# A channel shuffle in 44 DMAs: the first two buffers of each pool filled in small pieces

## The chip, the cores and the metric

The kernel runs on one core of a Trainium2 chip. The core has several engines with instruction streams of their own. Here VectorE (DVE in the profile) copies, SyncE (SP) issues the loads, ScalarE (ACT) issues the stores, and 16 DMA engines move the bytes of both. The metric is the device time of one execution in microseconds; the time before is the median of six runs.

## What is computed

The input holds 16 x 64 x 64 = 65,536 rows of 256 channels in float32, 64 MB. In each row the channels are seen as 8 groups of 32, and the two axes are exchanged: a channel shuffle, a pure move of data with no arithmetic.

```python
batch, h, w, c = x.shape                      # 16, 64, 64, 256
channels_per_group = c // groups              # 256 // 8 = 32
x = x.reshape(batch, h, w, groups, channels_per_group)
x = x.transpose(0, 1, 2, 4, 3)
x = x.reshape(batch, h, w, c)
```

Every byte is read from the chip's memory once and written once: 67.11 MB each way.

## The kernel before

The input is taken as one flat array. It is cut into consecutive chunks of 128 x q rows. Each of the 128 partitions of the on-chip memory gets q consecutive rows, that is q KB, since a row of 256 float32 is 1 KB. The list `_SIZES` (line 12) says which q are used: 4, 8, 16, then fifteen times 32, then 4. So there are 19 chunks, of 512 KB (q = 4), 1 MB, 2 MB, and 4 MB (q = 32) in all.

One loop runs over the chunks, and each pass does three things:

- line 47: SP issues one DMA that loads the chunk into `in_tile`;
- line 49: VectorE copies `in_tile` to `out_tile` with the two axes exchanged, through strided views;
- line 53: ACT issues one DMA that stores `out_tile` to the output.

`in_tile` comes from a pool of three buffers and `out_tile` from another pool of three. Every buffer has room for the largest chunk, 32 KB in each partition, and a chunk takes a whole buffer however small it is. Buffers are handed out in turn. So the load of chunk i waits until chunk i - 3 has been copied out of its input buffer, and the copy of chunk i waits until the store of chunk i - 3 has landed, besides the load of chunk i itself.

The order of the instructions is that of the loop (line 43 asks for a manual schedule); each engine goes through its own in that order. SP has 19 loads and ACT 19 stores, each 128 partitions by 1024, 2048, 4096 or 8192 float32 elements. The waits go over semaphores that the framework hands out: a completion semaphore for each DMA, taken in turn from a set of eight for loads and stores together, and one that counts VectorE's copies. A semaphore is used again for a later DMA, and the engine that issues that DMA waits first until the earlier one on the same semaphore has landed.

Of the kernel before, what the change touches and what calls it, by code (L numbers as in the profile page):

```python
# [1 line left out]

# [4 lines left out]


F32 = mybir.dt.float32
P = 128  # L10

_SIZES = [4, 8, 16] + [32] * 15 + [4]
_IN_BUFS = 3
_OUT_BUFS = 3


@with_exitstack
def kernel(
    ctx: ExitStack,
    tc: tile.TileContext,  # L20
    x: bass.AP,
    groups: bass.AP,
    out: bass.AP,
):
    nc = tc.nc
    b, h, w, c = x.shape
    G = int(groups)
    CPG = c // G
    assert G * CPG == c
    assert sum(_SIZES) * P == b * h * w  # L30
    biggest = max(_SIZES)

    x_flat = x.rearrange("b h w c -> (b h w c)")
    out_flat = out.rearrange("b h w c -> (b h w c)")

    in_pool = ctx.enter_context(tc.tile_pool(name="in_pool", bufs=_IN_BUFS))
    out_pool = ctx.enter_context(tc.tile_pool(name="out_pool", bufs=_OUT_BUFS))

    def rows(flat, first, q):

        return flat[first * c : (first + P * q) * c].rearrange("(p f) -> p f", p=P)

    ctx.enter_context(tc.manual_schedule(engines=None))
    first = 0
    for q in _SIZES:
        in_tile = in_pool.tile([P, biggest * c], F32, name="in_tile")
        nc.sync.dma_start(out=in_tile[:, : q * c], in_=rows(x_flat, first, q))  # L47
        out_tile = out_pool.tile([P, biggest * c], F32, name="out_tile")
        nc.vector.tensor_copy(  # L49
            out=out_tile[:, : q * c].rearrange("p (i j g) -> p i j g", j=CPG, g=G),  # L50
            in_=in_tile[:, : q * c].rearrange("p (i g j) -> p i j g", g=G, j=CPG),
        )
        nc.scalar.dma_start(out=rows(out_flat, first, q), in_=out_tile[:, : q * c])
        first += P * q


# [1 line left out]
_INS = ['x', 'groups']  # L58
_OUTS = [((16, 64, 64, 256), 'float32')]

_NUMBERS = {'groups': 8}


# [26 lines left out]
```

## Time and profile before

| | us |
|---|---|
| median of six runs | 316.74 (316.66 to 317.0) |
| the profiled execution | 316.7 |
| its span in the profile | 314.9 |
| VectorE busy, 19 copies | 120.1 |
| a copy of 128 x 8192 (32 KB), mean of 15 | 7.473 |
| a copy of 128 x 4096 / 2048 / 1024 | 3.841 / 2.010 / 1.096 |
| a 4 MB load from issue to landing, median | 50.5 |
| a 4 MB store from issue to landing, median | 42.1 |

The profile follows one execution. The span runs from its first to its last recorded event; the execution's own time is 1.8 us longer. Queue q1 carries the loads and q10 the stores. A transfer is cut into packets, one for each partition and a small one of 4 bytes for the completion on each of the 16 DMA engines, and the trace has a record of each packet with its size, start and duration. 5,472 packets in all move 134.22 MB, at a mean of 426 GB/s over the span. Times from issue to landing include the time that a transfer stands in its queue behind earlier ones.

### The profile page before, as it was taken

What the parts mean: (1) busy time and instruction counts of PE and PEld (TensorE: products, weight loads), DVE (VectorE), ACT (ScalarE), POOL (GpSimd) and SP (SyncE); (2) the same over time, 40 slices, a digit from 0 to 9 for tenths busy, and PEclk for the clock granted to TensorE, in tenths of its full rate; (3) what the DMA queues carried; (4) which work ended last, traced back from release to release, by engine and by line L of the source; (5) the groups of instructions that cost most, each with busy time, mean ns of one, the idle gap of its engine ahead of it and who ended that gap; (6) DMA issues with size and microseconds to landing.
All of it is one profiled execution on the core that took longest, in us unless ns stands there. A gap on an engine that the chain in (4) does not pass through costs nothing.

```text
span 314.9 us, 150 instructions
## 1 busy us (share of the span) xinstructions
DVE 120.1 (38%) x19; POOL 0.2 (0%) x4
## 2 busy tenths in 40 slices
DVE  3409270905318062170722608136080450905500
POOL 0000000000000000000000000000000000000000
DMA  8999999999999999999999999999999999999997
GB/s 318 405 427 444 408 458 404 462 404 462 404 462 404 462 404 462 404 462 404 466 400 466 400 466 400 466 400 466 400 466 400 466 400 466 400 466 427 439 400 333
DMA packets 5472, 134.22 MB, mean 426 GB/s; under 512 B 608, under 2 KB 608, under 8 KB 1120
## 3 DMA queue, kind: packets, MB, share of 16 engines
q1 hardware_dynamic: 2736, 67.11, 49.9%
q10 hardware_dynamic: 2736, 67.11, 49.4%
HBM read 67.11 MB, written 67.11 MB: 426 GB/s over the span
## 4 chain that ended last, share of the span: by engine, by line
DMA 40%; another core or an unknown queue 30%; DVE 25%; issue 0%; DVEq 0%; SPq 0%
DMA in_tile<-in_x_dram 40%; DVE out_tile L49 25%; DVEq L49 0%; SPq L47 0%
## 5 line engine op out<-in xcount | busy, mean ns | idle before, releaser
L49 DVE COPY out_tile<-in_tile 128x8192 f32<-128x8192 f32 (+3 forms) x19 | 120.1, 6323 | 179.2 <-DMA in_tile<-in_x_dram 179.2
L71 POOL MEMSET const-bfloat16-1.0<- 128x1 bf16 x1 | 0.1, 102 | 0.0
L71 POOL MEMSET const-uint8-127<- 128x1 uint8 x1 | 0.1, 102 | 0.0
L71 POOL MEMSET const-float32-0.0<- 128x1 f32 x1 | 0.1, 99 | 0.2 <-issue 0.2
L71 POOL MEMSET const-float32-1.0<- 128x1 f32 x1 | 0.1, 99 | 0.0
## 6 DMA issues: line engine op xcount, KB each, us to landing
in_tile<-in_x_dram SPq DMA_DIRECT2D x15, 4096.0 KB, 50.5
out_dram<-out_tile ACTq DMA_DIRECT2D x15, 4096.0 KB, 42.1
in_tile<-in_x_dram SPq DMA_DIRECT2D x1, 2048.0 KB, 11.0
out_dram<-out_tile ACTq DMA_DIRECT2D x1, 2048.0 KB, 29.9
in_tile<-in_x_dram SPq DMA_DIRECT2D x2, 512.0 KB, 22.6
in_tile<-in_x_dram SPq DMA_DIRECT2D x1, 1024.0 KB, 5.2
out_dram<-out_tile ACTq DMA_DIRECT2D x2, 512.0 KB, 14.4
out_dram<-out_tile ACTq DMA_DIRECT2D x1, 1024.0 KB, 23.2
```

The source lines that it names most:

```text
L49: nc.vector.tensor_copy(out=out_tile[:, : q * c].rearrange("p (i j g) -> p i j g", j=CPG, g=G), in_=in_tile[:, : q * c].rearrange("p (i g ...
L71: nc = _bacc.Bacc("TRN2", target_bir_lowering=False, num_devices=1)
```

## The change

`_SIZES` is replaced by `_SLOTS`, a list of buffers, each with a list of pieces. The first buffer of each pool is shared by six pieces of 4, 4, 4, 4, 8 and 8 KB per partition, the second by two of 16 KB, and fourteen more tiles of 32 KB follow. The small chunk at the end is gone. Each piece still has its own load, its own copy and its own store, on a part of the columns of the shared tiles. There are 22 of each, so 44 DMAs instead of 38.

Within one buffer the loop now issues all loads of its pieces first, and then goes through the pieces once more, with the copy and the store of each. A buffer is free for the tile that takes it next when all its pieces are done.

```diff
-_SIZES = [4, 8, 16] + [32] * 15 + [4]
+_SLOTS = [[4, 4, 4, 4, 8, 8], [16, 16]] + [[32]] * 14
...
-    for q in _SIZES:
+    for parts in _SLOTS:
         in_tile = in_pool.tile([P, biggest * c], F32, name="in_tile")
-        nc.sync.dma_start(out=in_tile[:, : q * c], in_=rows(x_flat, first, q))
         out_tile = out_pool.tile([P, biggest * c], F32, name="out_tile")
-        nc.vector.tensor_copy(
-            out=out_tile[:, : q * c].rearrange("p (i j g) -> p i j g", j=CPG, g=G),
-            in_=in_tile[:, : q * c].rearrange("p (i g j) -> p i j g", g=G, j=CPG),
-        )
-        nc.scalar.dma_start(out=rows(out_flat, first, q), in_=out_tile[:, : q * c])
-        first += P * q
+        at = 0
+        pieces = []
+        for q in parts:
+            pieces.append((q, first, slice(at * c, (at + q) * c)))
+            first += P * q
+            at += q
+        for q, start, cols in pieces:
+            nc.sync.dma_start(out=in_tile[:, cols], in_=rows(x_flat, start, q))
+        for q, start, cols in pieces:
+            nc.vector.tensor_copy(
+                out=out_tile[:, cols].rearrange("p (i j g) -> p i j g", j=CPG, g=G),
+                in_=in_tile[:, cols].rearrange("p (i g j) -> p i j g", g=G, j=CPG),
+            )
+            nc.scalar.dma_start(
+                out=rows(out_flat, start, q), in_=out_tile[:, cols]
+            )
```

In the built program of the changed kernel SP issues the loads in the order of the list, 1024 elements x4, 2048 x2, 4096 x2 and 8192 x14, VectorE copies and ACT stores in the same order. The first five loads wait for nothing. The sixth uses the semaphore of the second. The seventh and eighth (16 KB) and the ninth (the first of 32 KB) use the semaphores of the first, second and third store, and so wait for these to land.

More of the change, by code (lines that the diff above doesn't have):

```diff
@@ L29 @@
     assert G * CPG == c
-    assert sum(_SIZES) * P == b * h * w
-    biggest = max(_SIZES)
+    assert sum(map(sum, _SLOTS)) * P == b * h * w
+    biggest = max(map(sum, _SLOTS))
     x_flat = x.rearrange("b h w c -> (b h w c)")
```

## The prediction

> **What bounds the kernel now.** I read first the page's busy shares and its two DMA rows, then the same in stretches, then the ends of the run instruction by instruction.
>
> ```profile
> span 314.9 us, 150 instructions
> ...
> DVE 120.1 (38%) x19; POOL 0.2 (0%) x4
> ...
> DMA  8999999999999999999999999999999999999997
> GB/s 318 405 427 444 408 458 404 462 404 462 404 462 404 462 404 462 404 462 404 466 400 466 400 466 400 466 400 466 400 466 400 466 400 466 400 466 427 439 400 333
> ...
> q1 hardware_dynamic: 2736, 67.11, 49.9%
> q10 hardware_dynamic: 2736, 67.11, 49.4%
> ```
>
> The only engine that computes is busy 38% of the span. The two DMA queues, loads (q1) and stores (q10), fill 49.9% + 49.4% = 99.3% of the 16 DMA engines' time between them. The alternation 404/462 is only a beat of 4 MB transfers against slices.
>
> ```profile
> 1.70:5.00 3.30, 1.08 (x1) 0.00 (x0) 1.00 1.00 382
> 5.00:10.00 5.00, 2.03 (x2) 0.00 (x0) 1.00 1.03 388
> ...
> 100.00:260.00 160.00, 60.83 (x9) 0.00 (x0) 1.00 1.00 434
> 260.00:298.00 38.00, 14.97 (x2) 0.00 (x0) 1.00 1.01 435
> ...
> 312.00:314.90 2.90, 0.00 (x0) 0.00 (x0) 1.00 0.43 175
> ```
>
> (Columns: stretch, length, VectorE, GpSimd, clock, DMA share, GB/s.) The middle runs at 434 GB/s with a DMA share of 1.00. Below that rate are only the first microseconds and the last. So the kernel is bound by DMA work from its first packet (1.74 us in the packet records) to its last (313.66 us). VectorE's waits for loads cost nothing in themselves, as the DMA engines work through them.
>
> ```profile
> DVE out_tile L49 <- DMA in_tile<-in_x_dram: 179.2, 19, 12.0
> ...
> 3.92 1.09 DVE L49 COPY out_tile<-in_tile 128x1024 f32<-128x1024 f32 x1 [3.92 <-DMA in_tile<-in_x_dram]
> ...
> 5.05 57.66 ACTq L53 DMA_DIRECT2D out_dram<-out_tile  x6
> ...
> 287.25 7.51 DVE L49 COPY out_tile<-in_tile 128x8192 f32<-128x8192 f32 x1 [11.86 <-DMA in_tile<-in_x_dram]
> 298.24 1.10 DVE L49 COPY out_tile<-in_tile 128x1024 f32<-128x1024 f32 x1 [3.46 <-DMA in_tile<-in_x_dram]
> ```
>
> The first store is issued at 5.05 us. After the last copy, at 299.3 us, 14 us of stores still stand in the queue.
>
> **The account in packets.** A transfer gives each of the 16 engines 8 packets (128 partitions / 16), one per partition, and a 4-byte completion. Single packet records of this trace have a median of 0.159 us for 4 KB, 0.309 for 8 KB, 0.611 for 16 KB, 1.213 for 32 KB and 0.009 for the completion; thus some 0.009 us of a packet does not scale with its size. One engine's work in one direction before: 16 x 0.159 + 8 x 0.309 + 8 x 0.611 + 120 x 1.213 + 19 x 0.009 = 155.6 us, both directions 311.3. The page says 99.3% of 314.9 = 312.7 busy. The 1.4 us between are packets over their median, nearly all loads, and the records say when: 0.3 us up to 2.5 us (first accesses), 0.6 us from 5.5 to 9.9 us (16 KB loads with no store beside them, about 0.75 instead of 0.611 each), 0.5 us from 19 to 36 us (32 KB loads beside 8 and 16 KB stores), almost none later.
>
> **The change, part by part.**
>
> *More and smaller packets.* After: 32 x 0.159 + 16 x 0.309 + 16 x 0.611 + 112 x 1.213 + 22 x 0.009 = 155.9, both directions 311.7 us: +0.45. In the steady middle a 32 KB packet costs 32768 x 16 / 434 GB/s = 1.208 us, not 1.213, and 16 of these go: +0.08. Together +0.5 us; ends 0.4 and 0.6.
>
> The Trainium skill has a rule against this change ("DMA: Bandwidth & Descriptors", sections "Anatomy of one DMA" and "Rules for kernel authors"): about 2.0 us fixed per DMA, measured on the software-generated path, and at least 1 MiB each for bandwidth. Six more DMAs would be 12 us by it if nothing overlapped, 328.7 us in all; the packet records above have 9 ns per packet, because other transfers fill the wait.
>
> *The head.* Loads of 4, 4, 4, 4 and 8 KB go out unhindered. The first copy and store keep their rows (3.92 and 5.05 us), the next pieces follow at the pace of their loads (8 x 0.159 = 1.3 us against 1.09 us of copy). No transfer starts sooner than now, and there is no idle DMA to fill except the 1.74 us before the first packet, which stays.
>
> *The 16 KB loads no longer run alone.* Reads ahead of them: 32 x 0.159 + 16 x 0.309 = 10.0 us, from 1.74 + 0.3 on, so not before 12 us. The first store's packets begin between 6.1 (its issue plus the 1.0 us that the first load took from issue at 0.73 to packet at 1.74) and 9.1 us (where they began before). Up to then loads are of 4 and 8 KB, which ran at their median before. I take the 0.6 us off; ends 0 and -0.6.
>
> *The mix lasts longer.* The engines alternate one store packet with one load packet: the 512 KB store below takes 14.1 us to land, 8 packets of its own beside 16 and 32 KB loads.
>
> ```profile
> out_dram<-out_tile ACTq DMA_DIRECT2D x1, 512.0 KB, 14.1
> ```
>
> (The same page, section "Queues, rings and completion order", lets an engine drain a whole packet of about 9 to 17 descriptors before it switches; by that the 8 would go in one turn. The total would be the same by both.) Small stores before are 24 packets per engine, and 32 KB loads ran beside them from 12.6 to 45.5 us, 33 us, losing 0.5. After, 64 small store packets are paired with 64 loads. With loads some 32 packets ahead when stores begin, the last 32 pairs are 32 KB loads beside 16 stores of 8 KB and 16 of 16 KB: 32 x 1.213 + 16 x 0.309 + 16 x 0.611 = 53.5 us. At the same density that loses 0.5 x 53.5 / 33 = 0.8, so +0.3 us; ends -0.5 (no slow packets) and +2.3 (the density of the bad 9.5 us before, 0.5/9.5, over all 53.5 us = 2.8).
>
> *A wait that the diff does not show.* In the built program the DMAs share eight completion semaphores. The sixth load (8 KB) waits for the second one's landing, harmless at about 5 us. The two 16 KB loads and the first 32 KB load wait for the landing of stores 1, 2 and 3; all later loads stand behind them on SP, and then their copies and stores. Store 1 lands 8 x (0.159 + 0.309) + 0.35 = 4.1 us after its first packet, 10.2 to 13.2 us; the load's packets follow 1.05 us later. The load queue's own work lasts to 1.74 + 0.3 + 10.0 + 1.3 (store 1 between) = 13.3 us, so it may run dry for up to a microsecond. Then stores 2 to 4 (24 x 0.159 = 3.8 us) are copied already and keep the engines busy, and alone they land sooner. Cost nothing; without that cover 1.05 us for each of three loads, 3.2.
>
> *The middle.* Loads get further ahead (small stores get few bytes per turn), so a copy will wait for its output buffer's store rather than for its load, and loads will be issued as copies end. At such a copy's start two 4 MB stores are queued, 2 x 9.7 = 19.4 us of DMA work against a copy of 7.5. Cost nothing; uncovered it would be 7.5 us once.
>
> *The tail.* The final 512 KB tile goes; the last copy takes 7.5 us instead of 1.1 and its 4 MB store goes last. The 6.4 us are hidden by the same two stores. Before, 14 us of stores stood after the last copy; after, 19.4 + 9.7 - 7.5 = about 21. Cost nothing; uncovered 6.4 us.
>
> Sum: +0.5 - 0.6 + 0.3 = +0.2 us on the profiled execution. That one took 316.7 us, 314.9 of span and 1.8 around it, and the median of the six is 316.74. I add 0.2 to the median: 317.0 us, with rounding.
>
> **The rivals.** Two runs of this kernel are told apart from no change at about 0.2%, 0.63 us: faster is below 316.1, slower above 317.4.
>
> *Slow loads vanish.* Smaller stores sooner keep loads from running alone or against unlike partners, and only first accesses stay slow: 316.74 + 0.5 - 0.6 - 0.5 = 316.1, a little less if the first 0.3 shrinks too. For it: the steady state has none. Against: the 0.5 us came with small stores present, and there will be more of those.
>
> *The mix costs more (slower).* Place: 32 KB loads beside 8 and 16 KB stores, about 20 to 85 us. Price up to +2.3 instead of +0.3: 319.0; middle 318.0. It decides from 0.5 us above my term. For it: rows 20 to 36 us of the packet records. Against: from 12.6 to 19 us, beside 4 KB stores, there was no loss.
>
> *The semaphore waits leave both queues dry.* 1.05 to 3.2 us on top: 318.0 to 320.2. Against it: three or more stores are ready when the loads stall.
>
> **How the numbers follow.** My forecast, within 0.2%, has 0.45. Vanishing slow loads 0.22, the costly mix 0.25, dry queues 0.08. So faster 0.22, same 0.45, slower 0.33. The range leaves 0.1 on either side: below, 316.0, just under the fast rival's value; above, 318.6, midway in the costly mix. Between the ends of the unknown terms, 316.74 + 0.4 - 0.6 - 0.5 = 316.0 and 316.74 + 0.6 + 0 + 2.3 = 319.6, the upper part needs every bad end at once.
>
> **What would show it.** Two queues that fill 99% of the span again, with 434 GB/s in the middle; 3,168 packets (22 x 144) per queue; no load packet over its median between 6 and 10 us, some between 20 and 85 us; VectorE waiting for stores of out_tile as well as for loads; the first 16 KB load issued at 10 to 14 us; a last copy of 7.5 us with about 21 us after it. I am wrong if a stretch after 2 us shows a DMA share clearly under 1.00, if the middle's rate differs from 434, or if packets of 4 and 8 KB run far over their medians beside one another.

## The result, and the profile after

| | before | changed |
|---|---|---|
| median, us | 316.76 (36 runs) | 322.29 (16 runs) |
| shortest to longest, us | 316.56 to 317.22 | 317.80 to 329.14 |
| ratio, runs far above the shortest left out | 1 | 1.0095, interval 1.0073 to 1.0118 |
| profiled execution / its span, us | 316.7 / 314.9 | 318.3 / 316.6 |

The changed kernel is slower, and its time is no longer one number. Before, 36 runs lay within 0.7 us of each other (single later ones, taken beside the experiments, reached 317.3 to 318.2 us). After, 16 runs spread over 11 us. (The ratios, here and below, leave out runs more than 1.5% above the shortest of the same kernel.) The profiled execution is one of the short ones. First the page of the changed kernel, the rows that were read before:

```profile
span 316.6 us, 160 instructions
...
DVE 120.8 (38%) x22; POOL 0.2 (0%) x4
...
DMA  7999999999999999999999999999999999999996
GB/s 259 404 430 449 436 426 449 429 420 455 414 451 410 451 414 447 422 439 435 426 451 414 455 406 460 402 460 406 455 418 443 431 431 443 422 455 406 460 402 273
...
q1 hardware_dynamic: 3168, 67.11, 49.6%
q10 hardware_dynamic: 3168, 67.11, 49.3%
```

The DMA engines are as full as before: 98.9% against 99.3%, with 3,168 packets per queue as counted. The slices that fell are the first (318 to 259 GB/s) and the last (333 to 273). The same by stretches (length, VectorE, GpSimd, clock, DMA share, GB/s):

```profile
1.70:5.00 3.30, 0.93 (x1) 0.00 (x0) 1.00 0.92 325
5.00:10.00 5.00, 2.85 (x4) 0.00 (x0) 1.00 0.98 346
...
100.00:260.00 160.00, 64.86 (x9) 0.00 (x0) 1.00 1.00 433
...
312.00:316.60 4.60, 0.00 (x0) 0.00 (x0) 1.00 0.32 135
```

The middle runs at 433 GB/s, as before. The first 10 us lost some (382 and 388 GB/s became 325 and 346), and the last stretch has become 1.7 us longer with little in it. The waits of VectorE and of SP, and the first and the last copy:

```profile
DVE out_tile L57 <- DMA in_tile<-in_x_dram: 179.0, 22, 12.0
...
SPq L55 <- DMA out_dram<-out_tile: 12.8, 3, 8.2
...
4.07 1.09 DVE L57 COPY out_tile<-in_tile 128x1024 f32<-128x1024 f32 x1 [4.07 <-DMA in_tile<-in_x_dram]
...
292.33 7.50 DVE L57 COPY out_tile<-in_tile 128x8192 f32<-128x8192 f32 x1 [11.90 <-DMA in_tile<-in_x_dram]
```

The second row is the wait that the diff did not show: three loads stood 12.8 us for the first three stores. VectorE still waits for loads alone, 22 times out of 22.

What no busy share shows is how far the 16 DMA engines are apart. Each engine reports its own completion of a transfer, so the trace has 16 landings for each. From these records, for some 4 MB loads and for the last store (us: first engine, median, last engine; "spread" is last minus first):

```
                          before                  changed (318.3 us)
a load near 93 us         92.2  93.3  93.6  1.4   89.8  95.1  98.6   8.9
a store near 103 us      102.9 103.0 104.5  1.7  103.4 107.1 113.9  10.5
last 4 MB load           285.8 286.9 287.2  1.4  283.4 288.7 292.3   8.9
last store               313.5 313.7 314.0  0.5  313.9 314.1 315.6   1.7
```

In the changed kernel the engines are 8.9 to 10.5 us out of step in the middle, while the core as a whole moves 433 GB/s. Thirteen engines end within 0.4 us of each other and three are late, the latest by 1.5 us against the median. A transfer has landed when the last engine has finished its share, and the kernel ends with the last engine.

### The profile page after: what moved, and what is told of

Read it like the earlier page. It is cut to its first block, busy times and chain, and to the rows that moved or that the text cites. A ratio compares the mean times of both kernels' runs of the same rounds, so it can differ in the third digit from the quotient of the medians.

```text
span 316.6 us, 160 instructions
## 1 busy us (share of the span) xinstructions
DVE 120.8 (38%) x22; POOL 0.2 (0%) x4
## 3 DMA queue, kind: packets, MB, share of 16 engines
q1 hardware_dynamic: 3168, 67.11, 49.6%
q10 hardware_dynamic: 3168, 67.11, 49.3%
## 4 chain that ended last, share of the span: by engine, by line
DMA 34%; another core or an unknown queue 34%; DVE 26%; SPq 0%; issue 0%; DVEq 0%
DMA in_tile<-in_x_dram 31%; DVE out_tile L57 26%; DMA out_dram<-out_tile 3%; SPq L55 0%; DVEq L57 0%
```

## The experiments

Seventeen runs follow: three of the changed kernel itself and fourteen of further kernels. A diff is against the changed kernel unless another one is named.

**The same again.** Three more profiles of the changed kernel. `same` was also timed.

> The changed kernel once more, to see how its time scatters and to get a second profile. Theory A (the DMA engines fall out of step in the head, and the one that is latest ends the run): times from 317.8 to above 322 us again; in the profile the 16 landings of one transfer lie several us apart in the middle (1.7 us in the kernel before, 10 us in the first profile of the changed one), and the last store's landings more than 0.5 us apart. Theory B (more and smaller packets cost a fixed sum): every run within 0.3 us of the others, packets over their median in sum by what the time is longer. Theory C (the missing small last piece leaves the end uncovered): the loss is one gap after the last load, about the same in each run.

Ten runs, 317.58 to 325.0 us, median 321.66; ratio 1.0087, interval 1.0047 to 1.0126. The profile is of a run of 317.69: spread in the middle 10.7 us, last store 1.0 us. A fixed sum (theory B) is excluded by the scatter alone.

> The changed kernel again, for a profile of one of its longer executions. If it takes over 320 us: the landings of the last store lie 3 us or more apart, or the DMA engines stand idle for some us between the last load's landing and the last store, and load packets over their 1.213 us median recur in the middle. If it takes about 318: last landings 1 to 2 us apart and no slow packets in the middle, as in its first two profiles.

> The same once more, with the same expectation: the time beyond 316.7 us is the lateness of the latest DMA engine at the last store, plus any idle time before that store is issued.

By luck one is long, 323.88 us, and one short, 317.61. Three stretches and the last copy of the short one, then of the long one:

```profile
100.00:200.00 100.00, 41.22 (x6) 0.00 (x0) 1.00 1.00 433
200.00:280.00 80.00, 31.28 (x5) 0.00 (x0) 1.00 1.00 434
...
300.00:310.00 10.00, 0.00 (x0) 0.00 (x0) 1.00 1.00 433
...
290.34 7.53 DVE L57 COPY out_tile<-in_tile 128x8192 f32<-128x8192 f32 x1 [11.81 <-DMA in_tile<-in_x_dram]
```

```profile
100.00:200.00 100.00, 37.72 (x6) 0.00 (x0) 1.00 1.00 428
200.00:280.00 80.00, 30.17 (x4) 0.00 (x0) 1.00 1.00 427
...
300.00:310.00 10.00, 7.58 (x1) 0.00 (x0) 1.00 0.72 311
...
300.63 7.58 DVE L57 COPY out_tile<-in_tile 128x8192 f32<-128x8192 f32 x1 [12.38 <-DMA in_tile<-in_x_dram]
```

Two things differ. In the middle the long one moves 427 to 428 instead of 433 to 434 GB/s, with a full DMA share: packets took longer. And between 300 and 310 us the engines are idle for 28% of the time, because the last copy begins 10.3 us later. Its load:

```
last load landed:   first 283.3  median 288.1  last 290.3   (317.61 us)
                    first 288.1  median 293.5  last 300.6   (323.88 us)
```

The copy waits for the last engine. When its store is issued at 308.2 us, the store before it had landed on twelve of the 16 engines by 306.9, so these had nothing left to move. The balance of the two runs, from their packet records (last packet 314.53 and 320.79 us, 6.26 apart): packets over their median 1.30 and 3.89 us on the mean of the engines, +2.6, of which loads 2.0; idle between the last loads and the last store 0 and 2.6, +2.6; latest engine at the last store, as spread of its landings, 1.0 and 1.9, +0.9.

**The end of the list alone.** `tail_only` has the small last piece moved to the head:

```diff
-_SLOTS = [[4, 4, 4, 4, 8, 8], [16, 16]] + [[32]] * 14
+_SLOTS = [[4], [4], [8], [16]] + [[32]] * 15
```

> Only the small last piece is gone: pieces 4, 4, 8, 16 KB and fifteen tiles of 32 KB, each in a buffer of its own, 19 loads and 19 stores as before. Theory A: 316.5 to 317.0 us, no scatter, landings of one transfer within 2 us. Theory B: 316.7 to 316.9. Theory C: as slow as the changed kernel, 318 to 322, with idle DMA after the last load.

317.56 to 318.74 us, ratio 1.0041 (1.0027 to 1.0056): neither of what theory A said nor of C. There is no idle DMA after the last load, but one engine or a few are 1.2 us late from the first 10 us on (spread 1.2 to 1.3 us in every later transfer, 1.2 in the last store). The second 4 KB piece is the suspect, and the next kernel leaves it out:

```diff
+_SLOTS = [[4], [8], [20]] + [[32]] * 15
```

> The small last piece alone is taken away and no small piece is added: 4, 8, 20 KB and fifteen tiles of 32 KB, each in its own buffer, 18 loads and 18 stores. If the missing last piece leaves the end uncovered: over 317.4 us and DMA engines idle after the last load. If the run before this one (317.65 us with a second 4 KB piece in the head) lost its 0.9 us to engines that were held up by small packets in the head: 316.4 to 316.9, landings of the last store within 0.6 us.

316.47 to 317.03 us in 10 runs, ratio 0.9992 (0.9982 to 1.0002); last landings 0.5 us apart. Taking away the small last piece costs nothing; what `tail_only` lost came with the second 4 KB piece (the 16 KB piece became 20 KB as well).

**The head alone.** `head_tail` keeps the last piece and has the shared head:

```diff
+_SLOTS = [[4, 4, 4, 4, 8, 8], [16, 12]] + [[32]] * 14 + [[4]]
```

> The shared head with the small last piece kept: 4, 4, 4, 4, 8, 8 KB in the first buffers, 16 and 12 KB in the second, fourteen tiles of 32 KB, and 4 KB at the end; 23 loads and 23 stores. Theory A: 318 to 322 us with scatter, as the changed kernel. Theory B: 317.3, no scatter. Theory C: 316.7 to 317.3, no scatter.

319.59 to 323.86 us, ratio 1.0138 (1.007 to 1.0207): the head carries the loss, and a small last piece does not protect from it. The profiled run, 323.3 us, shows the marks of the long one above: slow load packets (3.3 us on the mean of the engines over both queues), last store spread over 3.2 us, and idle DMA of 1.5 us between 300 and 310.

**Pieces in buffers of their own.**

```diff
+_SLOTS = [[4], [4], [4], [4], [8], [8], [16], [16]] + [[32]] * 14
```

> The same 22 loads and 22 stores in the same sizes and order, but each piece has a buffer of its own, so loads run at most three pieces ahead. Theory A, if the scatter needs loads that are far ahead of their stores: near 317.2 us, landings of one transfer within 2 to 3 us. Theory A, if the small packets alone put the engines out of step: 318 to 322 with scatter. Theory B: 317.3 without scatter. A loss of 1 us or so more where the small loads, waiting for copies, leave the DMA engines dry in the first 10 us.

318.91 to 328.44 us, ratio 1.0116 (1.0053 to 1.018), landings 4 to 6.5 us apart. It is not the sharing of a buffer, nor loads that run far ahead.

**The wait for stores taken out.** `raw_nogate` writes the same transfers and copies out by hand, with a semaphore of its own for each DMA:

```diff
+            if s >= _IN_BUFS and i == of[s][0]:
+                sync.wait_ge(copied, of[s - _IN_BUFS][-1] + 1)
+            sync.dma_start(...).then_inc(landed[i], 16)
```

> The changed kernel's transfers and copies in the same order, written out with a semaphore of its own for each DMA, so that the 16 KB loads and the first 32 KB load no longer wait for the first three stores. If these waits throw the engines out of step: 316.7 to 317.4 us, no scatter, landings of one transfer within 2 us in the middle. If the small packets alone do: 317.6 to over 322 with scatter, landings 5 to 12 us apart.

318.19 to 321.52 us, ratio 1.0045 (1.0028 to 1.0062), landings 1.3 to 7.4 us apart after 30 us. The scatter needs no such wait; three of five runs at 318.2 to 318.3 leave open whether the wait makes it worse. The profiled run is the long one: latest engine 4.1 us behind the first at the last store, packets over their median 3.7 us on the mean.

**Small loads or small stores.** `big_stores` loads and copies in pieces but stores 4 MB at once; `big_loads` does the reverse. Pieces are columns of one 4 MB block there.

```diff
-            nc.sync.dma_start(out=in_tile[:, cols], in_=rows(x_flat, start, q))
+            nc.sync.dma_start(out=in_tile[:, cols], in_=whole[0][:, cols])
...
+        nc.scalar.dma_start(out=whole[1], in_=out_tile[:, : at * c])
```

And `big_loads`:

```diff
+        nc.sync.dma_start(out=in_tile[:, : at * c], in_=whole[0])
...
+            nc.scalar.dma_start(out=whole[1][:, cols], in_=out_tile[:, cols])
```

> Loads and copies in small pieces as in the changed kernel (each a part of the columns of one 4 MB block, so 4 to 16 KB runs at a stride of 32 KB in memory), but one 4 MB store for each buffer: 22 loads, 16 stores, no small store. Theory: an engine that is a microsecond late with small store packets, each of which takes its turn with a load packet four to eight times its size, ends up 5 to 12 us behind in stores and ahead in loads. Then here the landings of one transfer stay within 3 us and the times within 0.5 us of each other, though one late engine may still add 1 us. If small loads alone make the scatter: 318 to 325 as before.

> The other half: one 4 MB load for each of the first two buffers, then copies and stores in small pieces as in the changed kernel: 16 loads, 22 stores, no small load. The first copy waits for 4 MB, some 11 to 13 us, in which loads run alone. By the same theory small stores beside 32 KB loads spread the engines if they are out of step by then: landings over 5 us apart and scattered times, 318 or more. If small loads are what does it: one time near 317.5 to 319 (loads alone run slower), no scatter.

`big_stores`: 320.08 to 320.27 us, no scatter, landings 0.7 to 0.8 us apart from 46 us on. `big_loads`: 316.95 to 321.6 us in 10 runs, landings 4 to 8 us apart. Of the two, then, it is the small stores that spread the engines; small loads alone do not. That `big_stores` is slow all the same was not expected. Its stretches around the end and its last copy:

```profile
304.00:308.00 4.00, 2.33 (x1) 0.00 (x0) 1.00 0.31 131
...
298.83 7.49 DVE L58 COPY out_tile<-in_tile 128x8192 f32<-128x8192 f32 x1 [11.91 <-DMA in_tile<-in_x_dram]
```

With no small stores the loads gain no lead. The last 4 MB load lands at 298.7 us (287.2 in the kernel before), the stores ahead of the last one end at 304.8, the copy at 306.3, and the engines stand idle for 3.2 us: the end is uncovered although all engines are in step.

**Equal sizes on both queues.** On top of `raw_nogate`, loads of the first six buffers cut to 8 KB at most:

```diff
+            part = min(q, 8) if s < 6 else q
+            for k in range(0, q, part):
```

> The kernel with a semaphore for each DMA (318.19 to 321.52 us), with its stores and copies unchanged, but the loads of the first six buffers cut into pieces of at most 8 KB per partition, so that the small stores never take turns with load packets much larger than themselves. 18 more loads cost 18 x 0.009 + 80 x 0.009 + 0.1, about 1 us at most. If the unequal turns spread the engines: landings of one transfer within 3 us in the middle, times within 0.5 us of each other, 317 to 318. If small packets in the head spread them whatever they are paired with: landings 5 us apart or more and times scattered over 2 us, 318 to 323.

319.99 to 322.73 us, ratio 1.0167 (1.0128 to 1.0205). (The cut makes 14 more loads, 36 instead of 22, not the 18 of the expectation.) The spread is smaller, 1 to 4.7 us, but the time is no better, so a smaller spread alone does not give the time back; and the times scatter still (one of 320.0, three near 322.6), though here the small stores had no large partners. Only the shortest run was profiled; what the 322.6 us are made of is not known.

**Fewer and larger pieces.**

```diff
+_SLOTS = [[8, 8, 16]] + [[32]] * 15
```

> One shared buffer with pieces of 8, 8 and 16 KB, then fifteen tiles of 32 KB, no 4 KB piece and no small last one: 18 loads and 18 stores. If the number of small stores beside large loads decides: landings 2 to 5 us apart, 316.7 to 318.5 us. If any sharing of the first buffer throws the engines out of step: over 318 with scatter as in the changed kernel. If the head of before was merely lucky: anything over 317.4.

316.74 to 319.97 us, median 317.26, ratio 1.0024 (1.0005 to 1.0043), landings 2.6 to 3.8 us apart. By the ratios, three pieces lose about a quarter of what eight do.

**A known lag, put into the steady kernel.** `late5`, against the kernel before, adds loads of data that nothing reads; what is computed stays.

```diff
+        if n in (3, 6, 9, 12, 15):
+            nc.sync.dma_start(
+                out=aside[:, :], in_=x_flat[: 2 * 3936].rearrange("(p f) -> p f", p=2)
+            )
```

> The kernel before, with five extra loads of two partitions by 15.7 KB, ahead of chunks 3, 6, 9, 12 and 15, to a buffer that nothing reads. Each keeps two of the 16 DMA engines busy for 15744/32768 x 1.213 = 0.58 us, 2.9 us in all, and adds 5 x 2 x 0.58 / 16 = 0.4 us to the mean. If the latest engine sets the time: 319.6 us, the last store's landings 2.4 to 3.4 us apart. If the mean work does: 317.1 us. If engines out of step draw further slow load packets in the middle: more than 320, and scattered.

324.16 to 332.55 us. So 2.9 us of work on two engines cost 7 to 16 us. In the profile two engines fall further behind in loads with each extra one; the last 4 MB load lands on 14 engines by 288.7 us and on the last at 301.5, and the engines are idle for 6.9 us between 300 and 310. At the last store all are in step again, within 0.2 us: the time went into waiting for the late load.

`tiny5` makes the extra loads small:

```diff
-                out=aside[:, :], in_=x_flat[: 2 * 3936].rearrange("(p f) -> p f", p=2)
+                out=aside[:, :], in_=x_flat[: 2 * 256].rearrange("(p f) -> p f", p=2)
```

> The kernel before with five extra loads of two partitions by 1 KB, in the same places as the 15.7 KB ones of the run before (324 to 333 us). Their work is 5 x 0.06 = 0.3 us on two of the 16 engines. Turn theory: an engine serves the two queues one packet at a time, so each extra data packet and each extra completion in the load queue gives the store queue a turn with a 32 KB packet; two turns are 2 x 1.21 = 2.4 us by which these engines' loads fall behind, 12 us after five, as with the 15.7 KB loads. Then the last big load lands 10 to 14 us later on two engines than on the others, the last copy comes late, and the time is 321 to 331 us. Work theory: 316.7 to 317.1 us.

328.17 to 329.33 us, ratio 1.0372 (1.0346 to 1.0398), with 0.3 us of extra work. Packets of a fifteenth of the size cost about as much. From the profile:

```profile
300.00:314.00 14.00, 7.89 (x2) 0.00 (x0) 1.00 0.39 169
...
306.11 8.44 DVE L55 COPY out_tile<-in_tile 128x8192 f32<-128x8192 f32 x2 [11.89 <-DMA in_tile<-in_x_dram]
```

The last 4 MB load landed on 14 engines by 284.6 us, on the other two at 305.9 and 306.0; the copy follows at 306.1. The lag is 21 us, more than the 12 that two turns for each extra load would make. Part of it grew where no extra load landed (8.1, 10.7 and 12.9 us behind the median at 82, 104 and 125 us), which the turns do not explain.

`even5` gives each of the 16 engines one such packet:

```diff
+                out=aside[:, :], in_=x_flat[: 16 * 256].rearrange("(p f) -> p f", p=16)
```

> The control: the same five extra loads in the same places, with the same waits, but 16 partitions by 1 KB, one packet on each of the 16 engines. Turn theory: all engines give the same turns away and stay in step: 316.7 to 317.3 us, landings of one transfer within 2 us. If the extra loads or the waits they bring cost the time, as slow as the run with two engines, 321 to 331.

320.95 to 333.92 us, ratio 1.0157 (1.0109 to 1.0206): my expectation of the control was wrong. In its profile (320.95 us) the engines are in step, landings 1.0 to 2.6 us apart from 230 us on, yet the end is uncovered:

```profile
300.00:307.00 7.00, 6.81 (x2) 0.00 (x0) 1.00 0.68 288
...
298.32 8.49 DVE L55 COPY out_tile<-in_tile 128x8192 f32<-128x8192 f32 x2 [11.94 <-DMA in_tile<-in_x_dram]
```

Here all 16 engines gave turns away, the whole load queue fell back, and the last 4 MB load landed at 298.2 instead of 287.2 us, 11 us later for 5 x 2.4 = 12 expected of two engines. The lag came in steps: against the kernel before, the 4 MB loads land 5.1 to 5.5 us late after the second extra load, 7.8 to 7.9 after the third, 10.5 to 10.6 after the fourth and 11.0 to 12.2 after the fifth. Most steps are thus near the 2.4 us of two turns, and between the extra loads next to nothing is added. It is the lead of the loads over the stores that counts, on its latest engine; a lag shared by all uses it up just as well.

The extra loads also move semaphores to other DMAs, so that loads wait for stores, which none did in the kernel before:

```profile
SPq L53 <- DMA out_dram<-out_tile: 57.7, 5, 14.0
SPq L49 <- DMA out_dram<-out_tile: 44.5, 4, 14.9
```

These waits did not hold up the data: from 17 us on, every load was issued 21 us or more before the load ahead of it had landed on its first engine, so the load queue was never empty.

`late1` is `late5` with one extra load instead of five:

```diff
-        if n in (3, 6, 9, 12, 15):
+        if n in (9,):
```

> One extra load of two partitions by 15.7 KB, ahead of chunk 9. Turn theory: two engines fall 0.58 + 2.4 = 3.0 us behind in loads, landings of the later loads 4 to 5 us apart; the stores that are still queued cover so much at the end, and the time is only the 0.58 us of work longer, 317.0 to 317.8 us. If any lag is passed on in full: 319.7.

317.28 to 318.51 us and one run of 320.65; median 317.59, ratio 1.0039 (1.0015 to 1.0062). From the extra load on, two engines land at 135.1 us where the median lands at 132.0: 3.1 us behind, for 0.58 + 2 x 1.21 = 3.0 expected. The end covers that, and most runs lose about the 0.58 us of work and a little more.

**Shorter copies at the end.**

```diff
+_SLOTS = [[4, 4, 4, 4, 8, 8], [16, 16]] + [[32]] * 12 + [[16]] * 4
```

> The changed kernel with its last two 32 KB tiles cut into four of 16 KB, each in a buffer of its own, so that the last copy takes 3.8 us instead of 7.5. In the long execution that was profiled the DMA engines stood idle for 2.6 us on the mean between the last load's landing and the last store. If that is a good part of what the long executions lose: the longest ones shorten by 2 to 4 us and the median falls from 322 to about 320, the short ones stay at 317.6 to 318.3. If the middle's slow load packets and the latest engine are all of it: median 321 to 323 as before.

322.05 to 332.71 us, median 324.16, ratio 1.0198 (1.017 to 1.0226). No gain. In its profile the last load's landings lie 11.4 us apart (300.5 to 311.9), and the engines are idle for 4 us between 310 and 320: the lag of the latest engine is larger than what a shorter copy saves. The kernel is no clean test, though: with pieces of 16 KB the stores queued ahead of the last one are half as long too, so that the cover shrinks with the copy.

## Why the prediction was wrong

I forecast 317.0 us, no change. The step that failed is the account in packets: it added up one engine's work, with the mean of the slow packets, as if the 16 engines were one. The time follows the latest engine, and after that the lead of the loads. With it failed the term of the tail, put at nothing because 19.4 us of stores would cover the last copy: in a short execution some 12 us did, in a long one 5 to 6, less than the copy takes.

For the short executions (profiled: 318.3 us, last packet 315.24 against 313.66 us before, +1.6) term by term:

- *More and smaller packets*, +0.5: by the same medians, which did not move, +0.45. Right.
- *16 KB loads no longer alone*, -0.6: wrong. They no longer are, but the 4 and 8 KB loads that ran in their place were held up instead: packets over their median before 10 us cost 1.16 us on the mean against 0.89, so +0.3. Single 4 KB packets took up to 1.3 us near 5 us. Nor is it running alone that slows loads: in `big_loads` 32 KB loads ran alone until the first store at 14.4 us, and from 2.5 to 12 us they kept to their median.
- *The mix lasts longer*, +0.3: wrong in sign. From 12 to 100 us almost no packet was over its median, -0.5; after that some were, +0.1. The two errors nearly cancel: slow packets came to -0.1, where I had -0.3. That is luck.
- *The wait that the diff does not show*, 0: the first 16 KB load was issued at 14.1 us, at the late end of what I gave, and the load queue did run dry, near 17 us, with stores to move. As a cost of its own it was nothing. Engines did stand idle near 5 us; over the whole run idle time before the end came to about 0.2 us more.
- *The middle*, 0: right in time (433 GB/s). But no copy waited for its output buffer: all 22 waits were for loads, as before.
- *The tail*, 0: right in short executions, but with less cover than I counted. When the last copy began, at 292.3 us, the stores ahead of its own ran on until 304.2 to 305.9 us, some 12 us and not 19.4; after the copy 15.4 us were left and not about 21.
- Not in the sum: the latest engine at the last store, 1.3 us behind the mean of the 16 (1.5 behind their median) where it was 0.3, so +1.0.

Together +0.45 - 0.1 + 0.2 + 1.0 = 1.55, against 1.6 measured.

The long executions, and with them the median of 322.3 us, lose more: in the one of 323.88 us, against the short one of 317.61, 2.6 us of slow packets, nearly all in the middle and three quarters of them loads, 2.6 us of idle engines before the last store and 0.9 us more of the latest engine. The uncovered copy was in the prediction as a price (6.4 us for the tail), but I took two whole stores as cover, on every engine. A copy that waits for its load finds less of them left, and the later the last engine lands that load, the less: in the long execution the last copy began at 300.6 us, and on twelve engines the stores ahead of its own were done between 305.5 and 306.9 us, before the copy was (308.2 us).

Of the rivals, the costly mix had the right sign and the wrong place: beside small stores after 12 us slow packets are nearly gone, and those of the long execution come between 100 and 290 us beside 32 KB stores. Dry queues did not happen in the head. Vanishing slow loads did happen after 12 us, and did not help.

What is shown: the head causes it (`head_tail`, `tail20`), small stores, and several of them, make the scatter (`big_loads` has it, `big_stores` has not, `shared3` has less), a late engine costs far more than its work (`late5`, `tiny5`), and the last load's latest landing is what leaves the end idle. What stays open: why load packets in the middle slow down in some executions and not in others. A spread of 8 us alone does not do it, since the run of 317.61 us has that and not one slow packet there. Nor is it shown why a few engines are held up near 5 us.

No version beat the kernel before; the one without its small last piece equals it with 36 DMAs instead of 38.

## What to carry to other kernels

A kernel that fills its DMA engines to 99% can still lose to their disorder: look at the first and the last landing of single transfers, not only at busy shares, before adding small transfers to a head. Let the loads run well ahead of the stores, and count as cover at the end only what is still queued when the last load has landed on its latest engine. Time such a kernel in many runs, since a change that leaves the mean work alone can turn a steady time into a scattered one.

## What the runs showed of the hardware that was not expected

A DMA engine takes turns between the load and the store queue by single packets, whatever their size. One extra load of two partitions put two engines 3.1 us behind in loads (`late1`), two turns with a 1.21 us store packet and its own 0.58 us; packets of 1 KB on all engines put the loads back by about 2.5 us each time (`even5`). The Trainium skill ("DMA: Bandwidth & Descriptors", section "Queues, rings and completion order") has the engine drain a whole packet of about 9 to 17 descriptors before it switches; for rows of 4 KB and more these runs show one row for a turn.

Engines out of step stay so while both queues have work: in the run of 317.61 us the spread of a store was 8.2 us at 37 us and 7.9 at 260 us, and only when the loads were done did they close up, to 1.0 us. In the profile of `raw_nogate` the load queue ran dry on nearly all engines from 95 to 100 us; there the spread fell from 7.4 us, for a load near 95 us, to 1.3, for the store near 102 us, before it grew again to 4.1.
